# Token rows by 32x32 block transposes and a DRAM scratch, in place of TensorE transposes

## The chip, the core and the metric

The kernel runs on one core of a Trainium2 chip. The core has TensorE (PE in the profile, with its weight loads as PEld), VectorE (DVE), ScalarE (ACT), GpSimd (POOL, unused here), SyncE (SP, which here only issues DMAs) and 16 DMA engines. SBUF and PSUM are its on-chip memories, DRAM the device's. The metric is device time in microseconds for one execution. Everything is computed in float32.

## What is computed

The program is one inference step of a two-layer network (DEPTH 2, width 2048) for two groups of tokens at once: 256 prompt tokens and 32 sample tokens, 288 in all. Cut to what matters here, one layer is

```python
h = rmsnorm(x, norm_g)
q, k, v, gr, u, vm, gm, ar, am = split(h @ w_in)     # 1024,1024,2048 x 7 columns
q, k = rotary(q), rotary(k) * DK ** -0.5
o, s_new = retention(q, k, v, s0)                    # 8 heads, DK 128, DV 256
r_branch = (silu(gr) * head_groupnorm(o)) @ w_ret_out
vn = layernorm(gelu(vm), ln_g, ln_b)
m = gelu(u) * (W_s @ vn + bias)                      # W_s mixes token positions, per channel group
m_branch = (silu(gm) * m) @ w_mlp_out
x = x + (sigmoid(ar) * r_branch + sigmoid(am) * m_branch) @ w_o
```

Retention multiplies scores by decays and by v summed over tokens, and returns a state, the sum over tokens of decayed k times v, for each head. Outputs are the final normed tokens of both groups, the states and vn of the sample tokens.

The projection leaves channels on the partitions and tokens along the rows. Three results have to be summed over tokens, or normalised along channels for one token: V, VM and K. For these the kernel needs token rows: tokens on the partitions and channels along the row.

## The kernel before

**Pieces.** All weight matrices are cut into column pairs (256 columns, two tiles of 128). A pair is a job, and a job has four pieces of 512 weight rows each. For each piece PE runs 24 matmuls into a PSUM tile `ps` of shape 128 x 2 x 288: four row blocks, two column tiles, three products. The three products (`mm3`, lines 110 to 113) make one product of float32 accuracy from two rounded parts: the rounded value ("hi", a copy on ACT, `to_hi`, line 104) and what rounding lost ("lo", a subtraction on DVE, `to_lo`, line 107). Weights arrive by SP DMAs of 512 KB as `raw` (four buffers) and become `whi` (five buffers, ACT, line 105) and `wlo` (four buffers, DVE, line 108).

**Order.** The order on every engine is the order in which the program issues its instructions, written by hand. The main loop (lines 733 to 776) issues for piece s: the cast of piece s + 4, the residual of piece s + 3, the weight DMA of piece s + 7, then the 24 matmuls of piece s, then one `tick()`. When a job's last piece is issued, its evacuation is started: a Python generator (`evac_vm`, `evac_v`, `evac_k` and so on) that issues its next part at each tick, up to its next `yield`. So a `yield` is a delay of one piece, and "tick 3" below means three pieces after the job's last one.

**Jobs of a layer.** 8 VM pairs; 8 times U and GM; 8 times AM and the MLP output; 4 times Q, K, V, GR, V, GR; 8 AR; 8 retention outputs; 8 final outputs. In layer 0 the pieces of the first two VM jobs are interleaved (line 616).

**From channels to token rows.** `scaled` (line 202) multiplies `ps` by the token scale of the RMS norm (`rsb`, the same value on all partitions). `fourfold` (line 120, ACT) copies the 32 sample tokens four times side by side to make a full block of 128. `tok_blocks` (line 207) has PE transpose six blocks of 128 x 128 through the identity into two PSUM tiles: two prompt blocks and one sample block for each of the two column tiles (lines 212 and 215). Then:

- `evac_vm` (line 219) applies GELU on ACT from PSUM into `vmt` (lines 237, 238) and takes layer-norm statistics on DVE (line 241). `sgu_gen` (line 261) normalises the rows after the last VM pair and runs the position mixing.
- `evac_v` (line 435) makes hi and lo of V's rows on ticks 1 and 2 and runs its first matmuls with V on tick 3 (line 458); the state goes out on tick 5. The old state `s0` is read once more on tick 4 (line 487).
- `evac_k` (line 387) scales K's rows by the decays while it makes hi and lo (lines 402, 408), and then computes the scores.

`pre_q` (line 375) loads the masks and the `s0` of the next two heads, two buffers each, at the start of each Q job, five pieces after the last piece of the odd head's V. `rs_gen` (line 163) computes the token scale with matmuls against ones and the identity (lines 173 to 186).

Of the kernel before, what the change touches and what calls it, by code (L numbers as in the profile page):

```python
# [9 lines left out]
F32 = mybir.dt.float32  # L10
# [5 lines left out]
P = 128  # L16
DM = 2048
# [25 lines left out]
def trunk(ctx: ExitStack, tc: tile.TileContext, a, o):  # L43
# [76 lines left out]
    def fourfold(x):  # L120
        z4 = st([P, 2, P], "z4", bufs=2)
        S.copy(out=z4.rearrange("p j (r t) -> p j r t", r=4),  # L122
               in_=x[:, :, TP:T].unsqueeze(2).to_broadcast([P, 2, 4, TS]))
        return z4
# [38 lines left out]
    def rs_gen(last=None):  # L163
        acc = state["acc2"][:, 0]
        parts = [acc]
        if last is None:
            V.tensor_tensor(out=acc, in0=acc, in1=state["acc2"][:, 1], op=ALU.add)
            yield
            yield
        else:  # L170
            parts.append(last)
        p = aux()
        PE.matmul(p[:, 0:3], ident, ones[:, 1:4], start=True, stop=False)
        for n, x in enumerate(parts):
            for b in range(3):
                PE.matmul(p[:, b:b + 1], x[:, BLK[b]:BLK[b] + P], ones[:, 0:1],  # L176
                          start=False, stop=(n == len(parts) - 1 and b == 2))
# [9 lines left out]
        if last is not None:  # L187
            state["rs"] = p[:, 0:T]
        else:
            rs = st([P, T], "rsb")  # L190
            S.copy(out=rs, in_=p[:, 0:T])
            yield
# [13 lines left out]

    def tok_blocks(z, z4):

        p0, p1 = aux(), aux()
        for b in range(2):  # L210
            for jj in range(2):
                PE.transpose(p0[:, b * 256 + jj * 128:b * 256 + jj * 128 + 128],  # L212
                             z[:, jj, b * 128:b * 128 + 128], ident)
        for jj in range(2):
            PE.transpose(p1[:, jj * 128:jj * 128 + 128], z4[:, jj], ident)  # L215
        return p0.rearrange("p (b c) -> p b c", b=2), p1[:, 0:256]


    def evac_vm(l, c, ps):
        if "rs" in state:  # L220
            z = scaled(ps)
        else:
            z = st([P, 2, T], "z", bufs=3)
            S.copy(out=z, in_=ps[:, :, 0:T])
            while "rs" not in state:
                yield
            V.tensor_tensor(out=z, in0=z, in1=bc2(state["rs"]), op=ALU.mult)
        if state.get("vml") != l:
            state["vml"] = l
            state["vmt"] = st([P, 3, DM], "vmacc")  # L230
            state["bst"] = st([P, 3, NPR, 6], "bst")
        vmt, bst = state["vmt"], state["bst"]
        z4 = fourfold(z)
        yield
        p0, p1 = tok_blocks(z, z4)
        sl = slice(c * 256, c * 256 + 256)
        S.activation(out=vmt[:, 0:2, sl], in_=p0, func=AF.Gelu)
        S.activation(out=vmt[:, 2, sl], in_=p1, func=AF.Gelu)
# [22 lines left out]
    def sgu_gen(l, g):  # L261
# [12 lines left out]
        to_hi(wq, wsk)  # L274
        sl = slice(g * 256, g * 256 + 256)
        for b in range(3):
            x = vmt[:, b, sl]
            V.scalar_tensor_tensor(out=x, in0=x, scalar=mvl[:, b, 0:1], in1=lg,
                                   op0=ALU.subtract, op1=ALU.mult)
            V.scalar_tensor_tensor(out=x, in0=x, scalar=r[:, b:b + 1], in1=lb,  # L280
                                   op0=ALU.mult, op1=ALU.add)
# [6 lines left out]
        vh, vl = st([P, 3, 256], "vh", F32R, bufs=2), st([P, 2, 256], "vl", F32R, bufs=2)  # L288
        to_hi(vmt[:, :, sl], vh)
        load(o["gv"][l, :, sl], vmt[0:TS, 2, sl])  # L290
        load_sgu(l, g + 1)
        yield
        to_lo(vmt[:, 0:2, sl], vh[:, 0:2], vl)
        to_lo(vmt[HALF, 2, sl], vh[HALF, 2], vh[HALF, 2])
        yield
# [4 lines left out]
        for d in range(2):  # L300
            p = aux().rearrange("p (b h i) -> p b h i", b=2, h=2)
            ds = slice(d * 128, d * 128 + 128)
            for b in range(2):
                PE.matmul(p[:, b], vh[:, b, ds], w2, start=True, stop=False)  # L304
                PE.matmul(p[:, b, 0], vl[:, b, ds], w2[:, 0], start=False, stop=True)  # L305
            PE.matmul(ps_[:, d * TS:d * TS + TS], vh[:, 2, ds], wsk, start=True, stop=True)  # L306
# [80 lines left out]
    def evac_k(l, hp, ps):  # L387
        yield from rotary(ps, "rk", "k")
        r, rh, rl = state["k"]
        q, qh, ql = state["q"]  # L390
        r4 = fourfold(r)
        yield
        p0, p1 = tok_blocks(r, r4)
        kh, kl = st([P, 3, 256], "kdh", F32R), st([P, 2, 256], "kdl", F32R)
        parts = []
        for b in range(3):
            for jj in range(2):
                cs = slice(jj * 128, jj * 128 + 128)
                src, dc, hi = p0[:, b, cs] if b < 2 else p1[:, cs], kdec[:, 2 * hp + jj, b:b + 1], kh[:, b, cs]
                parts.append((src, dc, hi, kl[:, b, cs] if b < 2 else None))  # L400
        for src, dc, hi, lo in parts:
            S.activation(out=hi, in_=src, func=AF.Copy, scale=dc)
        yield
        for src, dc, hi, lo in parts:
            if lo is None:
                src, dc, hi = src[HALF], dc[HALF], hi[HALF]
                lo = hi
            V.scalar_tensor_tensor(out=lo, in0=src, scalar=dc, in1=hi.bitcast(F32),
                                   op0=ALU.mult, op1=ALU.subtract)
        state["kd"] = (kh, kl)  # L410
        for jj in range(2):
# [19 lines left out]
            for src, hi, lo in parts:  # L431
                to_lo(src, hi, lo)
            state["w", h] = (wh, wl)

    def evac_v(l, h, ps):
        z = scaled(ps)
        z4 = fourfold(z)
# [4 lines left out]
        p0, p1 = tok_blocks(z, z4)  # L442
        vh, vl = st([P, 3, 256], "vh", F32R, bufs=2), st([P, 2, 256], "vl", F32R, bufs=2)
        to_hi(p0, vh[:, 0:2])
        to_hi(p1, vh[:, 2])
        yield
        to_lo(s0, s0h, s0l)
# [8 lines left out]
        jj = h % 2  # L456
        po, pq = aux(), aux()
        mm3(po[:, 0:256], wh[:, 0:128], wl[:, 0:128], vh[:, 0], vl[:, 0])
        mm3(po[:, 256:512], wh[:, 128:256], wl[:, 128:256], vh[:, 0], vl[:, 0], stop=False)
        mm3(po[:, 256:512], wh[:, 256:384], wl[:, 256:384], vh[:, 1], vl[:, 1], start=False)  # L460
        PE.matmul(pq[:, 0:256], w2s[jj], vh[:, 2], start=True, stop=False)
        mm3(pq[:, 0:256], qdh[jj], qdl[jj], s0h, s0l, start=False)
        bst = st([P, 3, 6], "gst", bufs=2)
# [417 lines left out]
```

## Time and profile before

| | |
|---|---|
| time, median of 3 runs | 2382.21 us (2382.1 to 2382.36) |
| time of the profiled execution | 2382.11 us |
| its span | 2380.3 us |
| PE busy | 2365.4 us, 17892 matmuls |
| DVE busy | 1389.3 us |
| ACT busy | 1025.5 us |
| DMA engines, mean busy share (queue 1) | 51.3% |
| DMA packets of queue 1 | 129936, 399.57 MB |

An engine counts as busy from the start to the end of its instructions; neighbours on PE overlap, so the listed length of a matmul is more than what it adds to the queue. An instruction that issues a DMA does not count as busy. A row of groups gives the line, the engine, what is written and read, the shapes, the count, and then the busy total in us, the mean length in ns, and the idle time of the engine just before these instructions with what ended it. In a timeline the first column is the start in us, the second the length.

### The profile page before, as it was taken

The numbers are of one execution on the slowest core, as the hardware profiler recorded it, in microseconds if no ns is written. First come the engines' busy times: TensorE is split into PE (matmuls) and PEld (weight loads), VectorE is DVE, ScalarE is ACT, GpSimd is POOL, SyncE is SP. The second block draws the span as 40 slices with busy tenths as digits, with TensorE's granted clock in tenths as the row PEclk, the third lists the DMA queues.
The fourth block names the chain that finished last, engine by engine and source line by source line (L and its number), as shares of the span: only waits on it lengthen the run. The fifth ranks groups of instructions, "written<-read, shape, count | busy, mean of one in ns | idle before, by whom it ended". The sixth has DMA issues, their size and how long they took to land.

```text
span 2380.3 us, 42818 instructions
## 1 busy us (share of the span) xinstructions
PE 2365.4 (99%) x17892; PEld 2363.9 (99%) x17892; DVE 1389.3 (58%) x2079; ACT 1025.5 (43%) x1316; POOL 0.2 (0%) x4
## 2 busy tenths in 40 slices
PE   9999999999999999999999999999999999999997
PEld 9999999999999999999999999999999999999997
DVE  7477664446666664455555777544466666544544
ACT  6345543334444443334443555433344444433342
POOL 0000000000000000000000000000000000000000
PEclk9999999999999999999999999999999999999998
DMA  6455544454545544456644655545545444454553
GB/s 238 156 185 173 189 161 165 164 167 155 179 143 172 172 151 164 163 168 194 210 159 157 194 172 175 166 163 166 178 150 167 163 155 162 156 167 161 168 196 115
DMA packets 130129, 402.30 MB, mean 169 GB/s; under 512 B 17040, under 2 KB 34704, under 8 KB 129936
## 3 DMA queue, kind: packets, MB, share of 16 engines
q1 hardware_dynamic: 129936, 399.57, 51.3%
q8 instruction: 140, 2.29, 0.4%
q14 instruction: 53, 0.43, 0.1%
HBM read 390.07 MB, written 9.44 MB: 168 GB/s over the span
## 4 chain that ended last, share of the span: by engine, by line
PE 99%; DVE 0%; DMA 0%; SPq 0%; ACT 0%; issue 0%; DVEq 0%
PE ps L113 31%; PE ps L112 31%; PE ps L111 31%; PE aux L112 1%; PE aux L113 1%; PE aux L111 1%; PE aux L212 1%; PE aux L304 0%; PE aux L215 0%; PE aux L504 0%; DMA raw<-in_w_in 0%; DVE vmacc L789 0%; PE aux L305 0%; PE aux L417 0%; PE aux L176 0%; PE aux L306 0%
## 5 line engine op out<-in xcount | busy, mean ns | idle before, releaser
L108 DVE TENSOR_TENSOR wlo<-raw,whi 128x1024 fp32r<-128x1024 f32 (+1 forms) x705 | 859.9, 1220 | 561.8 <-PE ps L113 375.6
L105 ACT CAST whi<-raw 128x1024 fp32r<-128x1024 f32 (+1 forms) x705 | 735.3, 1048 | 754.7 <-PE ps L112 589.4
L111 PE MATMUL ps<-Ah,whi 128*128 128x288 f32 x2816 | 834.0, 296 | 1.0 <-ACT whi L105 1.0
L113 PE MATMUL ps<-Ah,wlo 128*128 128x288 f32 x2816 | 831.4, 295 | 0.8 <-DVE wlo L108 0.8
L112 PE MATMUL ps<-Al,whi 128*128 128x288 f32 x2816 | 830.5, 295 | 0.0
L111 PE MATMUL ps<-Bh,whi 128*128 128x288 f32 x2784 | 824.9, 296 | 0.0
L113 PE MATMUL ps<-Bh,wlo 128*128 128x288 f32 x2784 | 824.2, 296 | 0.0
L112 PE MATMUL ps<-Bl,whi 128*128 128x288 f32 x2784 | 823.7, 296 | 0.0
L111 PEld LDWEIGHTS ps<-Ah,whi 128*128 128x128 f32 x2816 | 529.1, 188 | 1.4 <-ACT whi L105 1.4
L113 PEld LDWEIGHTS ps<-Ah,wlo 128*128 128x128 f32 x2816 | 528.7, 188 | 1.5 <-DVE wlo L108 1.5
L112 PEld LDWEIGHTS ps<-Al,whi 128*128 128x128 f32 x2816 | 528.7, 188 | 0.0
L112 PEld LDWEIGHTS ps<-Bl,whi 128*128 128x128 f32 x2784 | 524.0, 188 | 0.0
L111 PEld LDWEIGHTS ps<-Bh,whi 128*128 128x128 f32 x2784 | 523.2, 188 | 0.0
L113 PEld LDWEIGHTS ps<-Bh,wlo 128*128 128x128 f32 x2784 | 522.5, 188 | 0.0
L204 DVE TENSOR_TENSOR z<-ps,rsb 128x576 f32<-128x576 f32 x81 | 61.2, 755 | 107.9 <-PE ps L113 107.9
L476 ACT ACTIVATE on<-aux,gnb,gny 128x256 f32<-128x256 f32 x32 | 16.3, 561 | 64.4 <-DVE gnb L472 64.4
L467 DVE BATCH_NORM_STATS2 gst<-aux 128x6 f32<-128x256 f32 x48 | 17.5, 420 | 43.7 <-PE aux L113 43.7
L122 ACT COPY z<-z 128x256 f32<-128x256 f32 x32 | 13.0, 407 | 63.7 <-DVE z L204 59.5
L308 DVE TENSOR_TENSOR rqh<-aux,wh 128x256 f32<-128x256 f32 x32 | 13.4, 419 | 33.3 <-PE aux L305 33.3
L335 ACT ACTIVATE z<-z 128x576 f32<-128x576 f32 x16 | 11.0, 687 | 46.3 <-DVE z L204 46.3
L352 DVE TENSOR_TENSOR vmacc<-ps,z 128x576 f32<-128x576 f32 x16 | 12.1, 758 | 30.6 <-PE ps L113 30.6
L361 DVE TENSOR_TENSOR zu<-ps,cosr 128x576 f32<-128x576 f32 x16 | 12.1, 757 | 30.6 <-PE ps L113 30.6
(229 smaller groups left out, 1198.8 us busy)
## 6 DMA issues: line engine op xcount, KB each, us to landing
raw<-in_w_in SPq DMA_DIRECT2D x511, 512.0 KB, 4.6
raw<-in_w_mlp SPq DMA_DIRECT2D x64, 512.0 KB, 4.7
raw<-in_w_ret SPq DMA_DIRECT2D x64, 512.0 KB, 4.6
raw<-in_w_o SPq DMA_DIRECT2D x64, 512.0 KB, 4.6
c<-in_dmask SPq DMA_DIRECT2D x16, 208.0 KB, 5.1
vmacc<-in_x SPq DMA_DIRECT2D x8, 288.0 KB, 6.9
wh<-in_ws_b SPq DMA_DIRECT2D x16, 144.0 KB, 6.2
zu<-in_x SPq DMA_DIRECT2D x8, 288.0 KB, 2.9
```

Source lines behind the costliest of these rows:

```text
L105: S.copy(out=hi, in_=src)
L108: V.tensor_tensor(out=lo, in0=src, in1=hi.bitcast(F32), op=ALU.subtract)
L111: PE.matmul(out, lh, rh, start=start, stop=False)
L112: PE.matmul(out, lh, rl, start=False, stop=False)
L113: PE.matmul(out, ll, rh, start=False, stop=stop)
L122: S.copy(out=z4.rearrange("p j (r t) -> p j r t", r=4), in_=x[:, :, TP:T].unsqueeze(2).to_broadcast([P, 2, 4, TS]))
L204: V.tensor_tensor(out=z, in0=ps[:, :, 0:T], in1=bc2(state["rs"]), op=ALU.mult)
L212: PE.transpose(p0[:, b * 256 + jj * 128:b * 256 + jj * 128 + 128], z[:, jj, b * 128:b * 128 + 128], ident)
L308: V.tensor_tensor(out=x, in0=p[:, :, 1], in1=bs[:, 0:TP].rearrange("p (b i) -> p b i", b=2), op=ALU.add)
L352: V.tensor_tensor(out=state["acc"][:, c], in0=ps[:, :, 0:T], in1=state.pop(("sig", c)), op=ALU.mult)
L467: V.bn_stats(out=bst[:, b], in_=src[b])
L476: S.activation(out=on[:, b], in_=src[b], func=AF.Identity, bias=nb[:, b:b + 1], scale=y[:, b:b + 1])
```

## The change

The transposes on PE go, for VM, V and K. In their place:

1. `put_tokens` (DVE, two instructions) transposes 32 x 32 blocks, straight from `ps` for VM and V, and from the rotated `r` in SBUF for K, into one SBUF tile `zt` (one buffer). The second instruction reads the 32 sample tokens four times.
2. `write_tokens` issues four DMAs on ACT's queue, one for each quarter of the partitions, which write the blocks into a DRAM tile `zd` (three buffers) so that the rows of a token come together. A run in DRAM is 32 floats.
3. `read_tokens` issues one DMA on SP's queue that reads the token rows back into SBUF: for VM into `vmt`, for K and V into `rows`, the free end of the tile that holds the MLP result.
4. V and VM are no longer multiplied by the token scale beforehand. `rst` holds that scale with tokens on the partitions, and the GELU of VM and the hi and lo of V take it as their scale.
5. V's first matmuls move from tick 3 to tick 5, VM's GELU from tick 1 to tick 4, K's hi and lo from ticks 3 and 4 to tick 6; K's scores come one tick earlier. `vmt`, `vh`, `vl`, `kh` and `kl` have the column tile as the outer index and the block as the inner one, so a V operand over both column tiles is two runs of 128.
6. In `rs_gen` the sample tokens of the first three scale computations are repeated four times by a DVE copy (`x4`), so that `rst` is right on all partitions. `fourfold` is left for K alone, with one buffer.

```diff
+    def put_tokens(zt, src):
+        V.transpose(out=zt[:, :, 0:8], in_=src[:, :, 0:TP].rearrange("p j (b t) -> p j b t", t=TS))
+        V.transpose(out=zt[:, :, 8:12], in_=src[:, :, TP:T].unsqueeze(2).to_broadcast([P, 2, 4, TS]))
+
+    def write_tokens(zt):
+        zd = dr.tile([24, 32, 4, 32], F32, name="zd", tag="zd", bufs=3)
+        for q in range(4):
+            S.dma_start(out=zd[:, :, q].rearrange("x t c -> t x c"),
+                        in_=zt[32 * q:32 * q + 32].rearrange("p j b c -> p (j b) c"))
+        return zd
+
+    def read_tokens(zd, dst):
+        load(dst.rearrange("p j b c -> p (j b) c"), zd.rearrange("(y b) t a c -> (b t) y (a c)", b=4))
...
     def evac_vm(l, c, ps):
...
+        zt = st([P, 2, 12, TS], "zt")
+        put_tokens(zt, ps)
+        yield
+        zd = write_tokens(zt)
+        yield
+        if c == 0:
+            state["vmt"] = st([P, NPR, 2, 3, P], "vmacc")
+        vmt = state["vmt"]
+        read_tokens(zd, vmt[:, c])
+        yield
+        yield
+        while "rs" not in state:
+            yield
         for b in range(3):
-            V.bn_stats(out=bst[:, b, c], in_=vmt[:, b, sl])
+            S.activation(out=vmt[:, c, :, b], in_=vmt[:, c, :, b], func=AF.Gelu, scale=rst[:, b:b + 1])
+        yield
+        for b in range(3):
+            V.bn_stats(out=bst[:, b, c], in_=vmt[:, c, :, b])
...
     def evac_k(l, hp, ps):
...
-        p0, p1 = tok_blocks(r, r4)
...
+        zt = st([P, 2, 12, TS], "zt")
+        put_tokens(zt, r)
+        yield
+        zd = write_tokens(zt)
+        kf = state["rows"][:, 0]
         for jj in range(2):
...
+            if jj == 0:
+                read_tokens(zd, kf)
+        yield
+        kh, kl = st([P, 2, 3, P], "kdh", F32R), st([P, 2, 2, P], "kdl", F32R)
...
     def evac_v(l, h, ps):
-        z = scaled(ps)
-        z4 = fourfold(z)
+        jj = h % 2
+        zt = st([P, 2, 12, TS], "zt")
+        put_tokens(zt, ps)
         s0 = state.pop(("s0", h))
...
         yield
-        p0, p1 = tok_blocks(z, z4)
...
         to_lo(s0, s0h, s0l)
-        to_lo(p0, vh[:, 0:2], vl)
+        zd = write_tokens(zt)
+        yield
+        vf = state["rows"][:, 1 - jj]
+        read_tokens(zd, vf)
+        yield
+        yield
+        vh, vl = st([P, 2, 3, P], "vh", F32R, bufs=2), st([P, 2, 2, P], "vl", F32R, bufs=2)
+        for b in range(3):
+            S.activation(out=vh[:, :, b], in_=vf[:, :, b], func=AF.Copy, scale=rst[:, b:b + 1])
+        for b in range(2):
+            V.scalar_tensor_tensor(out=vl[:, :, b], in0=vf[:, :, b], scalar=rst[:, b:b + 1],
+                                   in1=vh[:, :, b].bitcast(F32), op0=ALU.mult, op1=ALU.subtract)
         for q in ODD:
-            to_lo(p1[q], vh[q, 2], vh[q, 2])
-        yield
-        while ("w", h) not in state:
+            V.scalar_tensor_tensor(out=vh[q, :, 2], in0=vf[q, :, 2], scalar=rst[q, 2:3],
+                                   in1=vh[q, :, 2].bitcast(F32), op0=ALU.mult, op1=ALU.subtract)
+        yield
+        while ("w", h) not in state or "kd" not in state:
             yield
```

More of the change, by code (lines that the diff above doesn't have):

```diff
@@ L75, in trunk @@
     mvl = st([P, 3, 2], "mvl")
+    rst = st([P, 3], "rstok")
     def load(dst, src):
@@ L120, in fourfold @@
     def fourfold(x):
-        z4 = st([P, 2, P], "z4", bufs=2)
+        z4 = st([P, 2, P], "z4")
         S.copy(out=z4.rearrange("p j (r t) -> p j r t", r=4),
@@ L167, in rs_gen @@
             V.tensor_tensor(out=acc, in0=acc, in1=state["acc2"][:, 1], op=ALU.add)
+            x4 = st([P, P], "wsr", bufs=2)
+            V.tensor_copy(out=x4.rearrange("p (r t) -> p r t", r=4),
+                          in_=acc[:, TP:T].unsqueeze(1).to_broadcast([P, 4, TS]))
             yield
@@ L175, in rs_gen @@
             for b in range(3):
-                PE.matmul(p[:, b:b + 1], x[:, BLK[b]:BLK[b] + P], ones[:, 0:1],
+                t = x4 if b == 2 and last is None else x[:, BLK[b]:BLK[b] + P]
+                PE.matmul(p[:, b:b + 1], t, ones[:, 0:1],
                           start=False, stop=(n == len(parts) - 1 and b == 2))
@@ L191, in rs_gen @@
             S.copy(out=rs, in_=p[:, 0:T])
+            S.copy(out=rst, in_=yb[:, :, 0])
             yield
@@ L205, in scaled @@
         return z
[L207 to L216, printed above, removed]
-    def evac_vm(l, c, ps):
-        if "rs" in state:
-            z = scaled(ps)
[L222 to L225, printed above, removed]
-                yield
-            V.tensor_tensor(out=z, in0=z, in1=bc2(state["rs"]), op=ALU.mult)
+    def put_tokens(zt, src):
+        V.transpose(out=zt[:, :, 0:8], in_=src[:, :, 0:TP].rearrange("p j (b t) -> p j b t", t=TS))
+        V.transpose(out=zt[:, :, 8:12], in_=src[:, :, TP:T].unsqueeze(2).to_broadcast([P, 2, 4, TS]))
@@ L350, in evac_mlp @@
         if c == 0:
-            state["acc"] = st([P, NPR, 2, T], "vmacc")
+            t = st([P, 8 * 768], "vmacc")
+            n = NPR * 2 * T
+            state["acc"] = t[:, 0:n].rearrange("p (c j t) -> p c j t", c=NPR, j=2)
+            state["rows"] = t[:, n:n + 1536].rearrange("p (n j b c) -> p n j b c", n=2, j=2, b=3)
         V.tensor_tensor(out=state["acc"][:, c], in0=ps[:, :, 0:T], in1=state.pop(("sig", c)), op=ALU.mult)
@@ L391, in evac_k @@
         r4 = fourfold(r)
+        zt = st([P, 2, 12, TS], "zt")
+        put_tokens(zt, r)
         yield
-        p0, p1 = tok_blocks(r, r4)
[L394 to L410, printed above, removed]
+        zd = write_tokens(zt)
+        kf = state["rows"][:, 0]
         for jj in range(2):
@@ L433, in evac_k @@
             state["w", h] = (wh, wl)
+            if jj == 0:
+                read_tokens(zd, kf)
+        yield
+        kh, kl = st([P, 2, 3, P], "kdh", F32R), st([P, 2, 2, P], "kdl", F32R)
+        for jj in range(2):
+            for b in range(3):
+                dc = kdec[:, 2 * hp + jj, b:b + 1]
+                S.activation(out=kh[:, jj, b], in_=kf[:, jj, b], func=AF.Copy, scale=dc)
+        for jj in range(2):
+            for b in range(3):
+                q = HALF if b == 2 else slice(0, P)
+                V.scalar_tensor_tensor(out=kl[:, jj, b] if b < 2 else kh[q, jj, b], in0=kf[q, jj, b],
+                                       scalar=kdec[q, 2 * hp + jj, b:b + 1],
+                                       in1=kh[q, jj, b].bitcast(F32), op0=ALU.mult, op1=ALU.subtract)
+        state["kd"] = (kh, kl)
     def evac_v(l, h, ps):
-        z = scaled(ps)
-        z4 = fourfold(z)
+        jj = h % 2
+        zt = st([P, 2, 12, TS], "zt")
+        put_tokens(zt, ps)
         s0 = state.pop(("s0", h))
@@ L455, in evac_v @@
         kh, kl = state["kd"]
-        jj = h % 2
+        if jj:
+            state.pop("kd")
         po, pq = aux(), aux()
[L458 to L462, printed above, removed]
+        v0, v1, u0, u1 = vh[:, :, 0], vh[:, :, 1], vl[:, :, 0], vl[:, :, 1]
+        pa, pb, pc = halves2(po[:, 0:256]), halves2(po[:, 256:512]), pq[:, 0:256]
+        mm3(pa, wh[:, 0:128], wl[:, 0:128], v0, u0)
+        mm3(pb, wh[:, 128:256], wl[:, 128:256], v0, u0, stop=False)
+        mm3(pb, wh[:, 256:384], wl[:, 256:384], v1, u1, start=False)
+        PE.matmul(halves2(pc), w2s[jj], vh[:, :, 2], start=True, stop=False)
+        mm3(pc, qdh[jj], qdl[jj], s0h, s0l, start=False)
         bst = st([P, 3, 6], "gst", bufs=2)
```

46 lines of the change are left out of this document (19 added, 27 removed).

## The prediction

> **What bounds the kernel now.** I read the first two parts of the page, then TensorE's (PE's) waits, then the groups of the lines that go.
>
> ```profile
> span 2380.3 us, 42818 instructions
> PE 2365.4 (99%) x17892; PEld 2363.9 (99%) x17892; DVE 1389.3 (58%) x2079; ACT 1025.5 (43%) x1316; POOL 0.2 (0%) x4
> PEclk9999999999999999999999999999999999999998
> DMA  6455544454545544456644655545545444454553
> q1 hardware_dynamic: 129936, 399.57, 51.3%
> ```
> ```profile
> engine line waited for: us in total, times, longest us
> PE aux L184 <- DVE z L98: 2.8, 1, 2.8
> PE aux L681 <- DVE ones L675: 1.0, 1, 1.0
> PE ps L111 <- ACT whi L105: 1.0, 2, 0.6
> PE ps L113 <- DVE wlo L108: 0.8, 3, 0.4
> PE aux L176 <- DVE acc L577: 0.2, 1, 0.2
> ```
>
> PE is 99% busy at the granted clock's ceiling and waits 5.8 us in all. The rest of the span's 15 us without PE is start and end, which the edit leaves. So the time is PE's list of instructions. Work on VectorE (DVE, 58%), ScalarE (ACT, 43%) or the DMA engines (51%) costs nothing until it makes PE wait, and an instruction taken off PE is worth what it advances PE's queue. The profiled execution took 2382.11 us, 1.8 more than its span; the median of the three runs is 2382.21, so one serves for the other.
>
> **What PE loses.** The edit deletes the helper with lines 212 and 215:
>
> ```profile
> L212 PE MATMUL aux<-ident,z 128*128 128x128 f32 x128 | 19.4, 274 | 0.0
> L215 PE MATMUL aux<-ident,z 128*128 128x128 f32 x80 | 15.3, 273 | 0.0
> L212 PE MATMUL aux<-ident,zu 128*128 128x128 f32 x32 | 4.8, 272 | 0.0
> ```
>
> 128 + 32 + 80 = 240 transposes: 6 for each of 16 VM, 16 V and 8 K pairs. Their 273 ns is a length in a pipeline; what counts is the distance between starts:
>
> ```profile
> 51.26 0.60 PE L212 MATMUL aux<-ident,z 128*128 128x128 f32 x4
> 51.70 0.38 PE L215 MATMUL aux<-ident,z 128*128 128x128 f32 x2
> 51.91 0.60 PE L212 MATMUL aux<-ident,z 128*128 128x128 f32 x4
> 52.35 0.38 PE L215 MATMUL aux<-ident,z 128*128 128x128 f32 x2
> 52.49 0.38 PE L111 MATMUL ps<-Ah,whi 128*128 128x288 f32 x1
> 52.71 0.29 PE L112 MATMUL ps<-Al,whi 128*128 128x288 f32 x1
> ```
>
> Without the twelve, L111 would start at 51.26 and L112 one ordinary distance (2365 us of PE by 17892 matmuls is 0.13) later, at 51.39, instead of 52.71: 1.32 us for twelve, 0.110 each. 240 x 0.110 = 26.4 us; I take **26.5**. The other matmuls keep their number and columns. The sum is 2382.1 - 26.5 = **2355.6 us**, if PE never waits for what comes in place of the transposes.
>
> **What DVE, ACT and SyncE (SP) gain.** No row shows a DVE block transpose. By elements, the nearest rows are these:
>
> ```profile
> L204 DVE TENSOR_TENSOR z<-ps,rsb 128x576 f32<-128x576 f32 x81 | 61.2, 755 | 107.9 <-PE ps L113 107.9
> L108 DVE TENSOR_TENSOR vl<-aux,vh 128x512 fp32r<-128x512 f32 x16 | 10.9, 683 | 0.0
> L467 DVE BATCH_NORM_STATS2 gst<-aux 128x6 f32<-128x256 f32 x48 | 17.5, 420 | 43.7 <-PE aux L113 43.7
> L280 DVE SCALAR_TENSOR_TENSOR vmacc<-vmacc,lny,c 128x256 f32<-128x256 f32 x48 | 23.3, 485 | 1.7
> L122 ACT COPY z<-z 128x256 f32<-128x256 f32 x32 | 13.0, 407 | 63.7 <-DVE z L204 59.5
> ```
>
> put_tokens is one instruction of 512 elements and one of 256: 0.683 + 0.420 = 1.1 us (between 0.9, all at L204's ns per element, and twice 1.1). For VM and V the 0.755 of L204 goes. DVE gains 40 x 1.1 - 32 x 0.755, with V's residuals as two of 0.485 for one of 0.683: about 25 us of its 990 idle. ACT loses 32 of 40 four-fold copies (0.407) and gets three GELUs or casts for two, and four DMA issues a pair. The residuals, the row tiles' layout, rst and the x4 copy are the same work elsewhere, at nothing beside PE. The issues and the landings:
>
> ```profile
> L78 SPq DMA_DIRECT2D out_sp<-so x16: 357/423/1323, 595.4 to 2061.9; - x16
> raw<-in_w_in SPq DMA_DIRECT2D x511, 512.0 KB, 4.6
> out_sp<-so SPq DMA_DIRECT2D x16, 128.0 KB, 4.4
> ```
>
> Four issues at 0.42 are 1.7 us of ACT a pair, 160 of them 68 us of its 1355 idle; if six times the descriptors cost six times the issue they are 10 us a pair, which is in rival C. SP gets 40 reads, 17 us.
>
> **The new wait.** A row set now goes PSUM, DVE, SBUF, four ACT DMAs, DRAM, one SP DMA, SBUF, casts. Call W the time from the first of the four issues to the landing of the last. The runs in DRAM are 32 floats, 128 bytes: 4 x 768 packets, 192 for each of 16 engines. The trace has one stretch with such packets alone, the loading of norm_g (128 packets of 128 bytes, and 16 completions):
>
> ```profile
> DMA packets 144, 0.02 MB, mean 33 GB/s; under 512 B 144, under 2 KB 144, under 8 KB 144
> q1 hardware_dynamic: 144, 0.02, 21.5%
> ```
>
> The stretch is 1.7 to 2.2 us: 0.215 x 0.5 x 16 / 144 = 12 ns a packet. 192 x 12 ns = 2.3 us, and W = 4.4 + 2.3 = **6.7 us**. Low end: the four issues alone, 4.4 + 3 x 0.42 = 5.7. High ends: if the stretch's half microsecond for 128 packets is a pace, 24 x 0.5 + 4.4 = 16; if a 128-byte write costs as much as the mean packet of the page (0.513 x 2380 x 16 / 129936 = 0.150 us), 192 x 0.150 + 4.4 = 33. I take 6.7 because the nearest row has packets of this very size. Bytes are not the matter: 40 x 2.9 us (write 2.3; read, 48 packets an engine at the same price, 0.6) is 5% of the engines' span beside 51%.
>
> The Trainium skill speaks against this move: DMA: Bandwidth & Descriptors, section Rules for kernel authors, says that a plain DMA with a rearranged access pattern is 19 times slower than the hardware transpose, and its section Specifications puts the smallest transfer at line rate at 512 bytes. No run here shows either for writes; the norm_g rows, reads of 128 bytes, show a short packet that is cheap.
>
> Who waits, for V, where PE uses the rows soonest (a tick is one piece, 24 matmuls x 0.132 = 3.2 us):
>
> ```profile
> 566.44 1.05 ACT L105 CAST whi<-raw 128x1024 fp32r<-128x1024 f32 x1
> 574.87 0.75 DVE L204 TENSOR_TENSOR z<-ps,rsb 128x576 f32<-128x576 f32 x1
> 575.54 1.21 DVE L108 TENSOR_TENSOR wlo<-raw,whi 128x1024 fp32r<-128x1024 f32 x1
> 585.35 0.28 PE L111 MATMUL aux<-vh,wh 128*128 128x256 f32 x1
> 585.47 0.28 PE L112 MATMUL aux<-vl,wh 128*128 128x256 f32 x1
> 604.38 0.76 DVE L204 TENSOR_TENSOR z<-ps,rsb 128x576 f32<-128x576 f32 x1 [1.91 <-PE ps L113]
> 614.39 0.29 PE L111 MATMUL aux<-vh,wh 128*128 128x256 f32 x1
> ```
>
> From evacuation to the first matmul on V: 585.35 - 574.87 = 10.5 for an even head, 614.39 - 604.38 = 10.0 for an odd one. The edit puts that matmul two ticks later, +6.4, and takes 0.66 of transposes out: 16.2 and 15.7 us. The chain: put 1.1, ACT 0.1, W, SP issue 0.4, read 5.1 (raw's 4.6 and 40 more packets an engine at 12 ns), hi 0.4, lo 0.5: W + 7.6. So PE does not wait while W is under 8.6 (even) and 8.1 (odd). The single zt buffer adds one condition: K's write is issued after the cast at 566.44, at 567.5, and V's put at 574.87 must find it landed: W under 7.4, else DVE stands still, and with it the weights' residuals queued behind, which are three pieces (9.6 us) ahead. At W = 6.7 all hold, by 0.7 us the closest. VM has four pieces, 12.8 us, between puts, and PE uses its rows only after the last; layer 0's first two VM jobs end two pieces apart, so DVE waits there 1.5 us once, inside the same lead.
>
> On SP the read stands before the raw loads and waits out W. The load behind it would go after the residual two ticks on, 2 x 3.2 + 1.2 = 7.6 us after the evacuation; the rows land at 1.2 + 6.7 = 7.9 and the read's issue takes 0.4: 0.7 us late. The next pair's s0 load (L381) needs the buffer that L487 reads, and L487 moves two ticks back while the load stays:
>
> ```profile
> 621.83 0.42 DVE L487 SCALAR_TENSOR_TENSOR so<-c,aux 128x256 f32<-128x256 f32 x1 [1.14 <-ACT so L486]
> 625.92 0.43 SPq L78 DMA_DIRECT2D c<-in_s  x1
> SPq L78 <- DVE wlo L108: 1885.5, 646, 7.6
> ```
>
> 621.83 + 6.4 = 628.2 against 625.9: the raw loads behind it go 2.3 us late. SP spends 1885 us waiting for DVE to free raw buffers, so a weight is loaded as early as buffers allow, three pieces ahead of its cast, which is four ahead of its use; 2.3 and 0.7 us disappear in that. I cost both at nothing; without that lead they would be 2.3 x 6 + 0.7 x 40 = 42 us.
>
> **The rivals.**
>
> B. *V's rows a little late.* For W over 8.0 an even head stalls (W - 7.4) + (W - 8.6), an odd one W - 8.1 once that is above zero: about 3W - 24.1 a pair of heads, 8 pairs. W = 8.5 gives 11 us back (2367), W = 9.1 all. For it: raw loads share the engines at 51%. Against: the landing of 4.4 includes that sharing. 0.14, a fifth of it within 0.2% of no change.
>
> C. *The scratch write is the bound* (slower). Same place, W over 9.1: PE waits at L111 on vh. W = 12 costs 8 x 11.9 = 95 us: 2451; W = 16 costs 191: 2547; W = 33 costs 599: 2955. For it: no row writes 128-byte runs, and 768 descriptors a DMA is six times anything here. Against: 12 ns. 0.17; 0.04 of this is W = 33, the case nearest to the skill's rule.
>
> D. *The strided operands pay.* V's 17 matmuls a head now read the moving operand as two runs of 128. If each ran like two matmuls of 128 columns at 0.110 instead of one at 0.12 (585.35 to 585.47), 16 x 17 x 0.10 = 27 us: 2383, no change. Against: 288 columns advance by 0.132 and 256 by 0.12, one rate by columns. 0.04, three quarters of it within 0.2%.
>
> E. *The edit frees the listed length*, 240 x 0.273 = 65 us: 2317. The starts above deny it. 0.02.
>
> **The numbers.** The forecast, 2355.6, has 0.63; its own range is 2352 (a little more freed at changes between transposes and matmuls) to 2360 (a few waits). Faster is 0.63 + 0.11 + 0.02 = 0.76, the same (within 0.2%, 4.8 us, about what a measurement of this kernel can tell from no change) 0.03 + 0.03, slower 0.17 + 0.01 = 0.18. The range runs from 2352 to 2384: it takes in B and D and leaves out C and E.
>
> **What would show it.** Right: L212 and L215 gone, PE busy about 2339, PE's waits still under 10 us, four ACT issues a pair landing within 8 us of the first. Wrong: PE waits of microseconds at L111 on vh, 8 or 16 times (B, C); DVE waiting for a DMA before put_tokens (W over 7.4); ACT issues of microseconds each; starts of the V matmuls over 0.12 apart (D).

## The result, and the profile after

| | before | changed |
|---|---|---|
| time, median | 2382.28 us (2382.1 to 2382.67) | 2364.85 us (2360.54 to 2367.49, 4 runs) |
| ratio to before | | 0.9924 [0.9912, 0.9936] |
| profiled execution | 2382.11 us | 2364.19 us |

The change saves 17.4 us. The forecast was 2355.6, so 9 of the 26.5 us that were to go have come back. And the runs, which lay within 0.6 us of each other, now lie 7 us apart: something in the kernel has begun to depend on chance.

The head of the page of the changed kernel, with the lines that answer to those shown of before:

```profile
span 2362.4 us, 42697 instructions
...
PE 2343.5 (99%) x17652; PEld 2340.0 (99%) x17652; DVE 1412.9 (60%) x2145; ACT 1023.2 (43%) x1315; POOL 0.2 (0%) x4
...
PEclk9999999999999999999999999999999999999998
...
q1 hardware_dynamic: 161808, 415.30, 53.9%
q10 hardware_dynamic: 125440, 15.74, 4.3%
...
PE 94%; DMA 3%; DVE 2%; issue 0%; ACT 0%; ACTq 0%; SPq 0%; DVEq 0%
```

PE has exactly 240 matmuls fewer (17892 - 17652) and is still 99% busy, but 2343.5 us and not the 2339 of the forecast. The new queue (q10) holds the 125440 packets of the scratch writes, 4.3% of the engines' span. In the last line, the chain that ended last, DMA now has 3% of the span. The new work itself, from the same page's groups and DMA issues (the last column there is the median from issue to landing):

```profile
L217 DVE STREAM_TRANSPOSE zt<-ps 128x512 f32<-128x512 f32 x32 | 22.9, 714 | 22.9 <-PE ps L114 18.3
L218 DVE STREAM_TRANSPOSE zt<-ps 128x256 f32<-128x256 f32 x32 | 13.0, 407 | 0.0
...
raw<-in_w_in SPq DMA_DIRECT2D x511, 512.0 KB, 4.7
...
zd<-zt ACTq DMA_DIRECT2D x160, 96.0 KB, 5.8
vmacc<-zd SPq DMA_DIRECT2D x40, 384.0 KB, 3.5
```

put_tokens costs 0.714 + 0.407 = 1.12 us (1.10 forecast). One scratch write of 96 KB takes longer to land than a weight load of 512 KB. PE's waits in the changed kernel:

```profile
PE aux L189 <- DVE z L99: 3.0, 2, 2.8
PE aux L318 <- DVE vl L109: 2.8, 2, 1.6
PE ps L112 <- ACT whi L106: 1.3, 2, 1.0
...
PE aux L489 <- DVE vh L474: 0.6, 2, 0.3
...
PE aux L112 <- ACT vh L469: 0.2, 1, 0.2
```

The sum of the view is 9.8 us against 5.8 before, just under the 10 that the prediction named. L189 is the token scale (2.8 of it is the end of the program, as before), L318 the first position mixing (SGU) of each layer, L489 and L112 belong to V. The rows of VM and V come up where one does not look first, in the waits of ACT, DVE and SP:

```profile
ACT vmacc L253 <- DMA vmacc<-zd: 52.6, 13, 5.5
DVE vl L471 <- ACT vh L469: 49.8, 16, 5.2
ACT vh L469 <- DMA vmacc<-zd: 47.1, 16, 5.0
SPq L79 <- DVE so L514: 30.4, 6, 5.6
```

(A row gives the us in all, the times, and the longest.) ACT stands at the GELU of 13 of the 16 VM pairs, 4.0 us each, until the rows are there, and at the casts of all 16 heads of V, 2.9 us each. The weights' casts are queued behind. So is the next pair's scratch write: for 13 of the 16 VM pairs it goes out 0.1 us after the GELU ahead of it has started, 1.8 to 4.5 us after the start of its own put, where the other three have 1.07. Late rows of one pair make the rows of the next one late.

**W.** The read is issued 0.02 to 0.16 us after the last write has landed, so W can be read off two timelines. For V of head 7 in layer 0, first the queue and the casts on ACT, then SP, then PE:

```profile
855.99 3.84 ACTq L223 DMA_DIRECT2D zd<-zt  x4
...
870.27 1.31 ACT L469 ACTIVATE vh<-vmacc,rstok 128x256 fp32r<-128x256 f32 x3 [4.97 <-DMA vmacc<-zd]
```
```profile
866.84 0.38 SPq L79 DMA_DIRECT2D vmacc<-zd  x1
```
```profile
870.38 0.29 PE L114 MATMUL ps<-Ah,wlo 128*128 128x288 f32 x1
870.83 0.38 PE L112 MATMUL aux<-vh,wh 128*128 128x256 f32 x1 [0.16 <-ACT vh L469]
```

W is 866.84 - 0.15 - 855.99 = 10.7 us here, and PE's matmul comes 0.32 us late (0.45 after the one ahead of it instead of 0.13). Worked out so for all 40 row sets of this profile, W has a median of 8.5 us (7.2 to 12.3), the read one of 3.5.

**A ledger.** One experiment below, b2, is the changed kernel without the scratch. Its 17652 matmuls stand in the same order, so the start of each can be subtracted from the start of the same one in the changed kernel. The difference grows in five places only (profiled executions, 2364.19 against 2355.78 us):

| place | the changed kernel falls behind by |
|---|---|
| start, 0 to 20 us | 0.2 us |
| token scale, 40 to 60 | 0.45 |
| end of VM and first SGU, layer 0, 140 to 160 | 3.85 |
| V, late heads (870, 1871, 2041) | 1.34 + 0.30 + 0.52 |
| end of VM and first SGU, layer 1, 1300 to 1320 | 1.57 |
| in all, with some hundredths elsewhere | 8.45 |

So 5.4 of 8.45 us are lost where the VM stage ends. There, in layer 0, ACT does this (ACTq lines are its DMA issues):

```profile
114.93 0.51 ACT L253 ACTIVATE vmacc<-vmacc,rstok 128x256 f32<-128x256 f32 x1 [3.99 <-DMA vmacc<-zd]
115.04 0.31 ACTq L223 DMA_DIRECT2D zd<-zt  x1
...
115.38 0.55 ACTq L223 DMA_DIRECT2D zd<-zt  x1
...
116.15 1.03 ACT L106 CAST whi<-raw 128x1024 fp32r<-128x1024 f32 x1
124.32 1.06 ACTq L223 DMA_DIRECT2D zd<-zt  x2
125.50 2.95 ACT L106 CAST whi<-raw 128x1024 fp32r<-128x1024 f32 x3 [8.32 <-PE ps L114]
130.73 1.31 ACT L253 ACTIVATE vmacc<-vmacc,rstok 128x256 f32<-128x256 f32 x3 [2.28 <-DMA vmacc<-zd]
```

The third write of the last VM pair is issued 8.9 us after the second, and from 117.2, when the cast at 116.15 ends, ACT does nothing: three weight casts come in a heap at 125.50. (The view puts this wait down to PE; but the issue at 124.32 stands ahead of those casts.) The records name the completion semaphore of each DMA. The DMAs of both queues take eight of them in turn, SP issued the five loads of the first SGU in this stretch, and so the third write was given the semaphore of the first and had to wait until that had landed. W is 12.3 us there, 11.7 at the same place of layer 1. What follows on DVE:

```profile
126.58 2.36 DVE L109 TENSOR_TENSOR wlo<-raw,whi 128x1024 fp32r<-128x1024 f32 x2 [8.14 <-ACT whi L106]
...
131.27 1.23 DVE L256 BATCH_NORM_STATS2 bst<-vmacc 128x6 f32<-128x256 f32 x3 [0.53 <-ACT vmacc L253]
...
140.42 2.35 DVE L109 TENSOR_TENSOR wlo<-raw,whi 128x1024 fp32r<-128x1024 f32 x2
142.69 0.68 DVE L109 TENSOR_TENSOR vl<-vmacc,vh 128x512 fp32r<-128x512 f32 x1
```

From the statistics at 131.27 on DVE works without a pause through the layer norm and the weights' residuals that have piled up, and the last input of the SGU, `vl`, is made at 142.69. In b2, without the scratch, the same two stand 4.6 and 4.8 us earlier, while the changed kernel's PE is only 0.65 us behind there:

```profile
126.66 1.07 DVE L248 BATCH_NORM_STATS2 bst<-vmacc 128x6 f32<-128x256 f32 x3
...
137.93 0.68 DVE L109 TENSOR_TENSOR vl<-vmacc,vh 128x512 fp32r<-128x512 f32 x1
```

In the changed kernel PE stands, and afterwards it is slow. The waiting matmul, then the windows of the changed kernel (sum of us, PE, PEld, DVE, ACT, POOL with their instructions, granted clock, DMA share, GB/s), then before's for the second stretch:

```profile
143.43 0.33 PE L318 MATMUL aux<-wsp,vl 128*128 128x128 f32 x1 [1.62 <-DVE vl L109]
```
```profile
141.00:144.50 3.50, 1.85 (x12) 1.38 (x12) 3.44 (x5) 2.60 (x3) 0.00 (x0) 1.00 0.49 158
144.50:148.00 3.50, 3.50 (x18) 3.50 (x18) 3.40 (x8) 1.62 (x2) 0.00 (x0) 0.53 0.63 113
```
```profile
144.50:148.00 3.50, 3.50 (x28) 3.50 (x28) 1.48 (x3) 3.17 (x4) 0.00 (x0) 1.00 0.59 239
```

The waiting matmul starts 2.0 us after the one before it (141.42), and the place costs almost 4: in the 3.5 us after the wait the granted clock is 0.53, and PE does 18 matmuls where it did 28. A wait row (1.62 here) shows less than half of that.

### The profile page after: what moved, and what is told of

It is laid out like the page before. It is cut to its first block, busy times and chain, and to the rows that moved or that the text cites. A ratio compares the mean times of both kernels' runs of the same rounds, so it can differ in the third digit from the quotient of the medians.

```text
span 2362.4 us, 42697 instructions
## 1 busy us (share of the span) xinstructions
PE 2343.5 (99%) x17652; PEld 2340.0 (99%) x17652; DVE 1412.9 (60%) x2145; ACT 1023.2 (43%) x1315; POOL 0.2 (0%) x4
## 3 DMA queue, kind: packets, MB, share of 16 engines
q10 hardware_dynamic: 125440, 15.74, 4.3%
## 4 chain that ended last, share of the span: by engine, by line
PE 94%; DMA 3%; DVE 2%; issue 0%; ACT 0%; ACTq 0%; SPq 0%; DVEq 0%
PE ps L113 30%; PE ps L114 30%; PE ps L112 30%; DMA zd<-zt 2%; PE aux L113 1%; PE aux L114 1%; PE aux L112 1%; DMA raw<-in_w_in 1%; DVE wlo L109 1%; DMA vmacc<-zd 1%; PE aux L317 0%; ACTq L223 0%; PE aux L531 0%; DVE vmacc L816 0%; ACT whi L106 0%
## 5 line engine op out<-in xcount | busy, mean ns | idle before, releaser
L112 PE MATMUL ps<-Ah,whi 128*128 128x288 f32 x2816 | 833.2, 296 | 1.3 <-ACT whi L106 1.3
L112 PE MATMUL ps<-Bh,whi 128*128 128x288 f32 x2784 | 823.5, 296 | 0.0
L112 PEld LDWEIGHTS ps<-Ah,whi 128*128 128x128 f32 x2816 | 529.6, 188 | 1.8 <-ACT whi L106 1.8
L112 PEld LDWEIGHTS ps<-Bh,whi 128*128 128x128 f32 x2784 | 523.1, 188 | 0.0
L210 DVE TENSOR_TENSOR z<-ps,rsb 128x576 f32<-128x576 f32 x52 | 39.4, 758 | 62.1 <-PE ps L114 61.5
L471 DVE SCALAR_TENSOR_TENSOR vl<-vmacc,rstok,vh 128x256 fp32r<-128x256 f32 x32 | 14.2, 484 | 49.8 <-ACT vh L469 49.8
L253 ACT ACTIVATE vmacc<-vmacc,rstok 128x256 f32<-128x256 f32 x48 | 21.0, 499 | 52.6 <-DMA vmacc<-zd 52.6
L469 ACT ACTIVATE vh<-vmacc,rstok 128x256 fp32r<-128x256 f32 x48 | 21.0, 501 | 47.1 <-DMA vmacc<-zd 47.1
L217 DVE STREAM_TRANSPOSE zt<-ps 128x512 f32<-128x512 f32 x32 | 22.9, 714 | 22.9 <-PE ps L114 18.3
```

The source lines that it names most:

```text
L112: PE.matmul(out, lh, rh, start=start, stop=False)
L210: V.tensor_tensor(out=z, in0=ps[:, :, 0:T], in1=bc2(state["rs"]), op=ALU.mult)
L217: V.transpose(out=zt[:, :, 0:8], in_=src[:, :, 0:TP].rearrange("p j (b t) -> p j b t", t=TS))
L253: S.activation(out=vmt[:, c, :, b], in_=vmt[:, c, :, b], func=AF.Gelu, scale=rst[:, b:b + 1])
L469: S.activation(out=vh[:, :, b], in_=vf[:, :, b], func=AF.Copy, scale=rst[:, b:b + 1])
L471: V.scalar_tensor_tensor(out=vl[:, :, b], in0=vf[:, :, b], scalar=rst[:, b:b + 1], in1=vh[:, :, b].bitcast(F32), op0=ALU.mult, op1=ALU.sub ...
```

## The experiments

**a0_after_again**: the changed kernel once more, to have its spread and to run beside the next three.

> The changed kernel itself, as the base of the other runs on this chip. Theory 1 (the 240 transposes were worth 26.5 us of PE's queue, and some 9 us are given back where rows come late: the first spatial-gating unit of each layer and a few V heads): 2360 to 2368 us, with a spread of several us between runs, because the landing times of DMAs decide. Theory 2 (the transposes were worth only 18 us, nothing is given back): 2364 to 2366 with a spread as small as before's, 0.6 us.

Measured: 2366.76 us (2364.03 to 2368.82, 5 runs), ratio 0.9933 [0.9919, 0.9947]. Its profiled execution (2366.66) is 10.9 us behind b2: 1.5 at the token scale, 5.5 and 3.2 at the ends of the VM stages, 0.5 at V. It shows where the token scale waits:

```profile
40.80 0.72 DVE L217 STREAM_TRANSPOSE zt<-ps 128x512 f32<-128x512 f32 x1 [3.35 <-DMA zd<-zt]
```

DVE stands 3.35 us at the second VM job's put, since the one `zt` is still being written out, and the arithmetic of the token scale is behind it in DVE's queue.

**a1_sgu_loads_early**: the five loads of the first SGU go out one pair earlier.

```diff
         read_tokens(zd, vmt[:, c])
+        if c == NPR - 2:
+            load_sgu(l, 0)
...
-        if g == 0:
-            load_sgu(l, 0)
```

> The five loads for the first spatial-gating unit of a layer are issued one tick before the last VM pair's evacuation instead of in the tick of its writes. Theory 1: the third write of the last VM pair no longer waits on a semaphore for the first to land, its W falls from about 12 us to 8 or 9, the 2.0 and 1.5 us waits of PE at the first unit of each layer go, and with the first of them the slow clock behind it: 2358 to 2361 us, 4 to 5 less than the changed kernel in the same call. Theory 2: no difference.

Measured: 2368.09 us (2364.04 to 2368.97), 0.9937 [0.9924, 0.9949]. The edit missed its aim: W of the last pair is 13.8 and 11.8 us, since its later writes now take the semaphores of the moved loads. Nothing follows about the theory.

**a2_v_one_tick_later**: V's casts, and all behind them, one piece later.

```diff
         read_tokens(zd, vf)
         yield
         yield
+        yield
```

> V's casts and first matmuls come one more tick (3.2 us) later. Theory 1: the waits of PE on V's rows (four heads, 2 us in the profile of the changed kernel) go: 1 to 3 us less than the changed kernel. Theory 2: no difference. A third possibility: SP's load of the next s0 waits 3.2 us longer for the odd head's last use of it, the weights behind it come late, and the kernel is slower than the changed one by up to 8 x 3 us.

Measured: 2364.49 us (2359.5 to 2369.07), 0.9924 [0.9911, 0.9936]. In the ledger V's share is gone, all of it; 1.4 stay at the token scale, and 4.7 and 0.35 at the ends of the VM stages. So late V rows do cost what the ledger says, 2.2 us in the first profile and 0.5 in a0, and this is too little to be seen between runs that lie 9.6 us apart.

**a3_both**: a1 and a2 together.

> The gating loads early and V one tick later together. Theory 1: both kinds of wait are gone, so nearly the whole of the forecast gain comes: 2356 to 2358 us, and the spread between runs falls below 2 us. Theory 2: as the changed kernel.

Measured: 2365.19 us (2361.26 to 2366.13), 0.9922 [0.991, 0.9935]. Token scale 3.7, ends of the VM stages 1.8 and 3.5, V none.

**b1_transposes_twice**: the kernel before, with the transposes of `tok_blocks` issued twice.

```diff
-        for b in range(2):
+        for _ in range(2):
+            for b in range(2):
...
```

> The kernel before with each of its 240 transposes run twice into the same place. By the distance of starts, 0.110 us each, it is 26.4 us slower: 2408 to 2409 us. If they are worth only what the change gained (theory 2), 2399 to 2400. By their listed length, 0.273 us, 2447.

Measured: 2408.63 us (2407.96 to 2408.79) against 2382.64, ratio 1.0108 [1.0091, 1.0125]: 26.0 us for 240 transposes more, 0.108 us each. The price on PE's queue is as forecast, and rival E (0.273 each, 65 us) falls.

**b2_no_scratch**: the changed kernel without the writes and reads. GELU, V's and K's casts read what lies in SBUF ahead of the scratch, so the rows are not the token rows; the first VM job has a `zt` of its own. All other instructions stay.

```diff
     def write_tokens(zt):
-        zd = dr.tile([24, 32, 4, 32], F32, name="zd", tag="zd", bufs=3)
-        for q in range(4):
-            S.dma_start(...)
-        return zd
+        return zt.rearrange("p j (b a) c -> p j b (a c)", a=4)
```

> The changed kernel without its 160 writes and 40 reads of the scratch: GELU and V's casts take the block-transposed tile itself, K's casts the untransposed r, so rows are not token rows and the outputs are not the reference's; every other instruction stands where it stood. Theory 1 (what was given back is waiting for the scratch): 2355 to 2357 us, spread under 1 us. Theory 2: 2363 to 2366, as the changed kernel.

Measured: 2355.98 us (2355.78 to 2356.49), 0.9888 [0.9873, 0.9902]. The head of its page:

```profile
span 2354.0 us, 42373 instructions
...
PE 2339.8 (99%) x17652; PEld 2338.1 (99%) x17652; DVE 1412.5 (60%) x2145; ACT 1026.9 (44%) x1315; POOL 0.2 (0%) x4
```
The sum of the prediction, 2355.6, is the time of the change without its scratch, to 0.4 us, with PE busy 2339.8 as forecast and waiting 5.2 us in all. The strided operands, the two put instructions, the moved ticks and rst cost nothing (rival D falls). The 9 to 11 us given back, and the spread (0.7 us here), belong to the scratch.

**b3_writes_twice**: every row set is written twice, to another DRAM tile first.

```diff
+        for d in (dr.tile([24, 32, 4, 32], F32, name="zx", tag="zx", bufs=3), zd):
+            for q in range(4):
+                S.dma_start(out=d[:, :, q]...
```

> The changed kernel with each scratch write issued twice, first into a second scratch that nobody reads, then into the right one. Theory 1: W, measured at 8.5 us, grows to 13 or 15, which is 3 to 5 us over what V's chain has room for, and VM's and K's writes hold zt longer: PE waits on V's rows at every head, 2430 to 2520 us. Rival (the rows are early enough by a wide margin, and PE's waits in the changed kernel had other causes): 2365 to 2370.

Measured: 2488.22 us (2483.97 to 2492.46, 2 runs), 1.0442 [1.0421, 1.0464]. From the first issue to the last landing it is 11.3 us in the median (13 to 15 expected), and ACT's eight issues alone take 7.3. PE's waits:

```profile
PE aux L112 <- ACT vh L470: 50.6, 14, 6.8
PE ps L112 <- ACT whi L106: 17.0, 12, 3.5
PE ps L114 <- DVE wlo L109: 10.0, 17, 0.7
```

2.8 us more of W, and 5.5 us more of ACT for each row set, turned a gain of 17 into a loss of 106. Rival C's place is real (V's first matmul, 14 of 16 heads). PE's waits add up to some 85 us more than before; with the clock down to a mean of 0.980 after them the loss is larger than the view says.

**c1_loads_spread**: the five loads of the first SGU go out one for each VM pair, two to six, so that they do not all stand between the same writes.

```diff
         read_tokens(zd, vmt[:, c])
+        if c == 2:
+            state["parts"] = parts_sgu(l, 0)
+        if 2 <= c <= 6:
+            next(state["parts"], None)
```

> The five loads for the first gating unit of a layer are issued one by one, one in each of the VM pairs 2 to 6, so that no DMA that the last VM pair's writes share a completion semaphore with is young. Theory 1a (W of the last VM pair is 12 to 14 us because its writes wait, one after another, for younger DMAs on the eight shared semaphores to land): W there falls to 8 to 10, PE's waits at the first gating unit of both layers and the slow clock behind them go, 4 to 6 us less than the changed kernel: 2358 to 2362. Theory 1b (the last VM pair is late whatever the loads do, since its LayerNorm chain is the longest): no difference, 2364 to 2368.

Measured: 2367.33 us (2365.8 to 2371.65), 0.9938 [0.9926, 0.995]. This time W of the last pair did fall, to 8.3 and 8.9, and no time was won: 5.0 and 1.6 us are lost at the ends of the VM stages, as before. But the rows came no earlier. In layer 0, W of the four pairs before rose from 8.6 to 9.7 us to 9.8 to 10.2, and the last pair's put came at 117.50 us instead of 112.76. The read of its rows, in the changed kernel and then in c1:

```profile
127.37 0.38 SPq L79 DMA_DIRECT2D vmacc<-zd  x1
```
```profile
130.41 0.38 SPq L79 DMA_DIRECT2D vmacc<-zd  x1
```

In layer 1 c1 reads them 1.1 us later (1296.86 against 1295.80). So a shorter W of the last pair alone wins nothing, and what the shared semaphores cost by themselves is not shown. DVE and PE in this run:

```profile
134.27 1.23 DVE L260 BATCH_NORM_STATS2 bst<-vmacc 128x6 f32<-128x256 f32 x3 [2.91 <-ACT vmacc L257]
...
139.73 1.22 DVE L109 TENSOR_TENSOR wlo<-raw,whi 128x1024 fp32r<-128x1024 f32 x1
```
```profile
141.00 0.40 PE L114 MATMUL ps<-Ah,wlo 128*128 128x288 f32 x1 [2.01 <-DVE wlo L109]
```

DVE waits 2.9 us for the GELU, then has the layer norm to do, and the residual of the weights that PE needs at once stands behind it.

**c2_own_first_tile**: the first VM job's `zt` is another tile, so the second does not wait for its write.

```diff
-        zt = st([P, 2, 12, TS], "zt")
+        zt = st([P, 2, 12, TS], "zt") if l or c else st([P, 2, 12, TS], "vh", bufs=2)
```

> The first VM pair of layer 0 gets a tile of its own for its transposed blocks, so that the second pair's block transposes do not wait on DVE until the first pair's writes have landed, with the token scale queued behind them. Theory 1: PE's wait at the token scale (0.4 to 2.1 us near 44 us in the profiles so far) goes: 0.5 to 2 us less than the changed kernel, 2362 to 2367, which may not be told from it. Rival: something else holds DVE there, no difference.

Measured: 2363.75 us (2360.72 to 2365.3), 0.9921 [0.9908, 0.9933]. The loss at the token scale is gone; 0.8 us turned up at 25 us instead.

**c3_all_three** (a2, c1 and c2) and **c4_two_without_v** (c1 and c2):

> Loads spread, own first tile, and V's casts and first matmuls one tick later. Theory 1a: all the places are covered, so the time is that of the kernel without the scratch (2356.0) within 2 us, 2355 to 2358, and the spread between runs falls to 1 us or 2. Theory 1b: 2361 to 2365.

> Loads spread and own first tile, V where the changed kernel has it. Theory 1a: as the run with all three, and 1 to 3 us more for the V heads whose rows come late: 2357 to 2361. If it equals the run with all three, V's rows were early enough and the later tick is worth nothing.

Measured: 2364.12 us (2360.08 to 2366.87), 0.9922 [0.9909, 0.9934], and 2365.59 us (2362.03 to 2368.26), 0.9928 [0.9914, 0.9942]. In c3 V loses nothing; the ends of the VM stages lose 4.6 and 5.0. In c4 they lose 4.6 and 1.1, V 2.5, and 1.2 us are lost at 100 us, inside the VM stage. In all of the kernels so far that have the scratch once and the GELU on tick 4, the two ends of the VM stage cost 5 to 10 us together.

These nine profiles can be put in order by the time at which the last VM pair's rows are read, less what the kernel has lost against b2 up to there. In layer 1 this goes from 1288.7 us with 0.35 us lost (a2) over 1289.9 with 1.6 (the changed kernel and c1) to 1293.4 with 5.0 (c3). In layer 0 the earliest, 126.1 (a3), loses 1.8, and the four latest, 128.3 to 129.2, lose 4.6 to 5.5. Not every step is in order, but the later the rows, the larger the loss.

**d1_rows_later**: more time for the rows of V and VM. V as in a2; the GELU of VM two pieces later; the first SGU after it, its loads after the last read, and the second SGU waits for the first.

```diff
         read_tokens(zd, vmt[:, c])
-        yield
-        yield
+        for _ in range(4):
+            yield
...
         if g == 0:
+            for _ in range(3):
+                yield
             load_sgu(l, 0)
+        while g == 1 and state.get("sgu0") != l:
+            yield
```

> Nothing is taken out. V's casts come one tick later, the GELU of VM two ticks later, and the first SGU step of each layer follows by as much: its five loads come after the last VM pair's rows have been read, and the second SGU step waits for the first. So every row set has 3.2 us (V) or 6.4 us (VM) more between its put and its first reader. Theory 1 (the 9 us given back are all waits for late rows, by PE directly or through ACT and DVE, which stand at a GELU or a cast with the weights' casts queued behind): with enough time for the rows the waits go everywhere except at the token scale near 44 us, and the kernel comes to within 1 to 3 us of the 2356.0 of the kernel without the scratch: 2356.5 to 2360, the waits of ACT for VM's rows (52.6 us in 13 waits) fall below 10 us, and the runs of this kernel lie within 2 us of each other. Theory 2 (a wait taken away comes back at the next reader or in the queues, as in the five kernels that moved one thing): 2363 to 2368, runs 4 to 9 us apart, with PE waits at other lines. Slower than 2370 would speak for a third cause, the first SGU step holding up GM.

Measured: 2361.35 us (2360.76 to 2366.27, 5 runs), 0.992 [0.9907, 0.9934]. The median is between the two expectations, and the runs lie 5.5 us apart, where theory 1 had 2. The one execution with a trace is the fastest of the five. ACT's 52.6 us at VM's GELU are gone, and of the 47.1 at V 0.4 are left. At the end of layer 1's VM stage PE loses nothing, at V nothing, at the former place in layer 0 0.2. The profiled execution (2360.76) is 5.0 us behind b2: 1.0 at the token scale, 0.3 at the start, and 3.4 at a new place, the second SGU of layer 0. DVE, PE and the granted clock there:

```profile
154.27 0.11 DVE L289 MEMSET wsr<- 64x64 f32 x1 [2.03 <-DMA wsr<-in_ws]
```
```profile
162.89 0.38 PE L321 MATMUL aux<-wsp,vh 128*128 128x256 f32 x1 [0.61 <-ACT vh L106]
164.03 0.33 PE L322 MATMUL aux<-wsp,vl 128*128 128x128 f32 x1 [0.75 <-DVE vl L109]
```
```profile
164.00:167.00 3.00, 2.98 (x18) 2.87 (x19) 2.90 (x6) 2.04 (x3) 0.00 (x0) 0.77 0.63 150
```

That wait is of the edit's own making: the loads of the second SGU are issued by the first, which now comes so late that DVE waits for them. So late rows are the cause at V (a2 moves nothing else) and at the end of VM: there b2, the order of the nine profiles and d1 say the same. d1 moves the GELU, the first SGU and its loads together; which of them is needed is not shown, nor that a schedule can come down to b2's time. d1 has the lowest median of the kernels with a scratch, but its interval overlaps that of the changed kernel: no version was measured to be faster.

## Why the prediction was right, and where it failed

The direction and the range held; the 2355.6 was 9 us too low. The forecast's own range, 2352 to 2360, did not hold. The stated one, 2352 to 2384, takes in the 2364.85 only because it has room for rivals B and D, and neither came as it was priced: that is luck. Of the signs of being right, PE's waits stayed under 10 us (9.8), but the writes landed 8.5 us after the first issue in the median, not within 8, and PE was busy 2343.5 us, not 2339.

**What bounds the kernel, and 240 x 0.110 = 26.5 us.** Right: 26.0 by b1, 26.7 by b2 (2382.64 - 2355.98).

**DVE, ACT, SP.** put_tokens as forecast; DVE is busy 1412.9 - 1389.3 = 23.6 us more (25). Four issues spread over 1.8 us (1.7). SP waits 30.4 us in six s0 loads behind L514, the wait that the prediction described; 5.1 us each is twice its 2.3, and it costs nothing, as it said: b2 has 42.7 us of the same wait.

**W and the read.** Two sizes were off and cancelled, by luck. W was 8.5, not 6.7. The short packets were not the reason: by q10's row they took 0.043 x 2362.4 x 16 / 125440 = 13 ns each (12). But one write of 96 KB took 5.8 us to land, where the sum had 4.4 for the landing, and the last write went out 1.8 us after the first. The read took 3.5, not 5.1. Together they are 12.0 us where the prediction had 11.8.

**V's lead.** Right in form. With the measured read the chain is W + 6.0, so PE waits for W over 10.2 (even head) or 9.7 (odd). In the profile, W is over its limit for three heads, all odd: 10.7, 9.8 and 10.0, 1.0, 0.1 and 0.3 us over; the ledger has 1.34, 0.30 and 0.52. Rival B foresaw 11 us given back for W = 8.5. It has the amount that was given back, at the wrong place: V's share is 0.5 to 2.5 us in the profiles that have V on tick 5.

**zt between K's write and V's put.** K's W was 7.4 to 7.8 us, just over the 7.4 allowed. DVE waited for a zt that was still being written twice in the profile, 3.8 us in all, but both times at a VM put of layer 0: 3.3 us for the second job and 0.4 for the fourth (at 62.11 us). At V's puts after K the view has no such wait.

**The step that failed** is "VM has four pieces, 12.8 us, between puts, and PE uses its rows only after the last". The prediction worked out the chain for V and not for VM. By its own numbers VM's rows land 1.1 + 0.1 + 6.7 + 0.4 + 5.1 = 13.4 us after the put, and the GELU stands at 12.8. It took a wait on ACT to be free because PE is not behind it. But ACT casts the weights in the same queue, and it issues the next pair's writes: the 0.1 us that the prediction had in V's chain for ACT between put and write became, for VM, 0.8 to 3.4 us in 13 of 16 pairs. After the last VM pair the layer norm stands in DVE's queue ahead of the residuals. In the middle of the stage the lead of three pieces covers that; at its end PE needs the rows themselves, the lead is used up, and in layer 0 the clock falls after the wait. This is 5.4 of 8.45 us in the first profile and 8.7 of 10.9 in a0. In d1, which gives these rows more time, the loss is gone in layer 1, and in layer 0 3.4 us stand at the second SGU.

**Layer 0's first two VM jobs.** "DVE waits there 1.5 us once, inside the same lead": DVE waited 3.3 us, and the token scale, which has no such lead, is behind it: 0.45 and 1.5 us of PE in the two profiles of the changed kernel, up to 3.7 in the others (a3).

**Rivals C, D, E.** D and E fall by b2 and b1. C is not what happened, but b3 shows its slope: 2.8 us more from the first issue to the last landing, and 7.3 us of ACT's queue a row set instead of 1.8, cost 123 us. The rule weighed in the prediction (the Trainium skill, DMA: Bandwidth & Descriptors, Rules for kernel authors) compares a plain DMA with a rearranged access pattern with the hardware transpose, which no run here has. What the runs have is the time of the rearranged DMAs themselves: 384 KB took 8.5 us to write in runs of 128 bytes, in four DMAs, and 3.5 to read in runs of 512, in one, a factor of 2.4. W = 33, which the prediction called nearest to the rule, is far from that.

What stays open: how much of the difference between runs of one kernel (5 to 10 us) each place has, since only one execution of each has a trace; what the shared semaphores cost by themselves; and why the last write of a set lands later than 1.8 + 5.8 us after the first issue.

## What to carry to other kernels

Work out the chain of a moved result for every reader, not only for the one on the bottleneck engine: a reader that waits on an in-order queue holds up what is queued behind it, here the weights that PE needs next. Where a wait is taken away and the median stands still, subtract the start times of the same matmuls in a version without the suspect; that ledger named the places, where the medians of seven edits had told nothing. And leave room for the tail: V had 13.2 to 13.7 us for the 12.0 that write and read took in the median, and in the first profile three heads of 16 were late all the same.

## What the runs showed of the hardware

- After a matmul that started 2.0 us after the one before it, the granted clock was 0.53 in the next window of 3.5 us (matmul starts 0.24 us apart, not 0.133). After 1.46 us between two starts at 1310 us it did not fall: it was 1.00 up to 1318, and the ledger has 1.57 there. The Trainium skill (TensorE: Matmul & The Clock Gate, Part 1) gives half clock after an idle window of about 3.4 us that does not start with the wait; the half agrees, while here 2.0 us between two starts were enough.
- The issue of a DMA on ACT's queue took 0.31 us for the first of four and up to 3.2 for a later one (shortest, median and longest in ns, of all 160):

```profile
L223 ACTq DMA_DIRECT2D zd<-zt x160: 309/608/3224, 32.2 to 2027.2; - x160
```

- DMAs of two queues took the same eight completion semaphores, and one held up another through them: 8.9 us between the second and the third issue of one row set, the third one 0.02 us after the first write, with the same semaphore, had landed in full (124.30).
